# Two queues and two due times in a decoder layer: gate loads through POOL, pooled loads in ACT's order, two late channels

## The chip, the core and the metric

The kernel runs on one core of a Trainium2 chip. The core has a matrix engine (TensorE, PE), VectorE (DVE), ScalarE (ACT), GpSimd (POOL) and SyncE (SP), and 16 DMA engines that move data between its memories and HBM. Each engine takes its instructions in a fixed order; SP, ACT and POOL also issue DMAs, each from its own queue, in that order. The metric is the device time of one execution in microseconds, the median of several runs.

## The reference

One decoder layer over 1024 tokens with 2048 channels, in float32. One projection makes queries, keys, values, two gate channels sets and the pooled branch; two token mixers work on it; each branch is gated by a SiLU; an output projection and a gated embedding follow, and a layer norm.

```python
h = jnp.einsum('bsd,dc->bsc', x, w_in) + b_in
q, k, v, g_attn, u_pool, g_pool = jnp.split(h, SPLIT_POINTS, axis=-1)
a = banded_sink_attention(q, k, v, sinks, bias_hqk, valid) * jax.nn.silu(g_attn)
b = multiscale_pool(u_pool, w_pool, pool_scale) * jax.nn.silu(g_pool)
mix = jnp.einsum('bsc,cd->bsd', jnp.concatenate([a, b], axis=-1), w_out)
ple = jax.nn.sigmoid(jnp.einsum('bsd,de->bse', x, w_gate_ple)) * jnp.einsum('bsp,pd->bsd', p_i, w_ple)
return layer_norm(DEEPNORM_ALPHA * x + mix + ple, ln_gain, ln_bias)
```

`multiscale_pool` has four groups g of 256 channels with trailing windows of 2, 4, 8 and 16 tokens: window mean less the token itself, then a 256x256 map per group (w_pool) and a scale per channel.

## The kernel before, in words

**Products.** A float32 matrix product is made from high and low parts: each operand is cast to fp32r (`wh`, ACT, L222) and the rest is taken by a subtraction (`wl`, DVE, L122), and three matmuls stand for one (high by high L179, low by high L180, high by low L181). Activations are split in the same way into sets of operands b11, b21, t1, t2, t3, b22, t4 (`split_unit`, L242 to L250). The seven operands are those of a scheme with seven block products instead of eight. Each job makes two blocks of 128 output channels in such seven products; one product is 12 matmuls of 128x512. Where two jobs form a pair, their products alternate (14 products). Banks `qa` and `qb` of the accumulators are emptied by a copy on ACT (L346) or an addition on DVE (L348, shown as L122).

**Order.** After each product `tick` counts one up. `after(n, f)` calls f at the n-th product from now; `later(n, f)` does the same and also holds f's instructions behind the newest of PE, ACT and DVE. A scheduler then fixes the order of each engine's queue from the order of the code and its own costs. So a due time in products is a place in five queues.

**The stages around the change.** The second half of the projection's jobs comes last in its stage: gates and pooled channels (gp0, u0 in a pair; then gp3, u3, gp2, u2, u1, gp1), eight jobs of the embedding's gate (wgate), and the attention's gates ga0, ga1 and the pair ga2, ga3. When such a job ends (`finished`), POOL issues an accumulating load that adds the first half's sum (`part<-h`, or `part<-g` for wgate; L359), and `wait` products later `done` runs for each of its two channels:
- `gate_attn`: a Silu on ACT (L597), four products with `s<-pre` (loads of the attention's result) on DVE, and a store into `cc` on POOL's queue (`aside`, L141).
- `gate_pool`: a Silu (L604) and a store into `sgp` on SP's queue.
- `pool_u`: the window sums (ACT, DVE), and for the second channel of a group the loads of w_pool and of the gates `s<-sgp` (by `fetch` on SP's queue, L136), and `mix` with its matmuls (`sc`), the product with the gates (L653) and four stores into `cc` on POOL's queue.

The output projection reads `cc`: its pooled half (`cc4` to `cc7`, eight loads of 512 KB, `two<-cc`, L267) is loaded by `set_from`, whose steps then make the seven operands; this runs during ga1 and the pair ga2, ga3. The attention's half comes later in the same way. Waits of a DMA on a buffer or on a semaphore lane hold all that stands behind it in its issuer's queue.

Of the kernel before, what the change touches and what calls it, by code (L numbers as in the profile page):

```python
# [32 lines left out]
T = 512  # L33
# [21 lines left out]
class Job:  # L55


    def __init__(self, w, b0, b1, half, first, done, tokens=2 * T, plain=False, ahead=None):
        self.ahead, self.filled, self.mean, self.wait = ahead, False, False, 4
        self.w, self.b, self.half, self.first, self.done = w, (b0, b1), half, first, done  # L60
        self.tokens, self.plain = tokens, plain


class Layer:
# [74 lines left out]
    def aside(self, out, src):  # L139

        self.nc.gpsimd.dma_start(out=out, in_=src)  # L141

    def fetch(self, src, extra=False):
        s = self.extra() if extra else self.slot()
        return self.load(s[:, : src.shape[-1]], src)
# [109 lines left out]
    def set_from(self, get, F, keep=None, first=None, by=None):  # L255
# [4 lines left out]
        def fetch(u, part=None):  # L260
            h, k = int(u[2]) - 1, 2 * (int(u[1]) - 1)
            if not part:
                r[u] = [self.two() for _ in range(2)]
            for i, t in enumerate(r[u]):
                src = get(h, k + i)
                if part is None:
                    (by or (nc.sync if first else nc.scalar)).dma_start(out=t, in_=src)  # L267
                elif i == 0 and part < 2:
                    self.load(t[:, part], src[:, part])
                elif i == 1 and part == 2:  # L270
                    self.load(t, src)
# [13 lines left out]
        def begin():  # L285
# [4 lines left out]
            for i, u in enumerate(("b11", "b21", "b12", "b22")):  # L290
                self.later(1 + 2 * i, lambda u=u: fetch(u))
# [62 lines left out]
    def finished(self, job, i, t):  # L354
# [7 lines left out]
        self.later(job.wait, lambda: job.done(job.b[i], t))  # L362
# [245 lines left out]
    def pool_u(self, j, c):  # L608
# [24 lines left out]
        if j % 2:  # L633
# [4 lines left out]
            self.after(6 + late, lambda: self.got.update({("sg", g): [[self.fetch(self.sgp[2 * g + e][:, h * T : h * T + T]) for e in range(2)] for h in range(2)]}))  # L638
# [201 lines left out]
    def run(self):  # L840
# [63 lines left out]
        for j in s3:  # L904
            j.wait = 3 if j in s3[-2:] else 4
            j.ahead = self.embed_ahead if j.w is wgate else (lambda b: self.gate_ahead(b - GA0)) if j.b[0] < U0 and j.wait == 4 else None
        mixed = [(wout, *p) for p in pairs(0, 8)]
# [116 lines left out]
        pooled, *make_pooled = self.set_from(lambda h, k: self.cc[4 + k][:, :, h * T : h * T + T], T, by=nc.sync)  # L1024
        for i in range(n3):
# [7 lines left out]
            if i == n3 - 2:  # L1033
# [8 lines left out]
                for n, step in enumerate(make_pooled):  # L1042
                    self.after(10 + 3 * n, step)
# [187 lines left out]
```

## Time and profile before

| | |
|---|---|
| median of 3 runs | 1488.71 us (1487.96 to 1489.05) |
| the profiled execution | 1488.72 us |
| its span, first to last instruction | 1486.9 us |
| PE busy | 1447.6 us, 97% of the span |
| DVE, ACT, POOL busy | 1118.7 (75%), 779.5 (52%), 278.1 us (19%) |
| mean granted TensorE clock | 0.992 of full speed |

Busy time is what an engine worked; it says nothing on what it waited for. A busy PE is one whose matmuls follow each other. A row with "[2.21 <-ACT part L346]" tells that the engine stood idle for 2.21 us before it and that this ACT instruction ended the wait. L numbers are lines of the kernel before.

### The profile page before, as it was taken

The numbers are of one execution on the slowest core, as the hardware profiler recorded it, in microseconds if no ns is written. First come the engines' busy times: TensorE is split into PE (matmuls) and PEld (weight loads), VectorE is DVE, ScalarE is ACT, GpSimd is POOL, SyncE is SP. The second block draws the span as 40 slices with busy tenths as digits, with TensorE's granted clock in tenths as the row PEclk, the third lists the DMA queues.
The fourth block names the chain that finished last, engine by engine and source line by source line (L and its number), as shares of the span: only waits on it lengthen the run. The fifth ranks groups of instructions, "written<-read, shape, count | busy, mean of one in ns | idle before, by whom it ended". The sixth has DMA issues, their size and how long they took to land. (4 is left out here: it accounts for less than half of the span.)

```text
span 1486.9 us, 20458 instructions
## 1 busy us (share of the span) xinstructions
PE 1447.6 (97%) x6972; PEld 1223.5 (82%) x6972; DVE 1118.7 (75%) x2019; ACT 779.5 (52%) x1548; POOL 278.1 (19%) x388
## 2 busy tenths in 40 slices
PE   8999999999999999999999999999999999999996
PEld 6788888888887888888887778888877788899986
DVE  7788578888797878888667956565669666987786
ACT  5454666655666555666534443333256333554485
POOL 0000123332332333231111110000011111111231
PEclk9999999999999999999999999999999999999998
DMA  7563875445545455457856676666696768585464
GB/s 264 198 226 94 254 207 183 149 158 179 174 170 178 163 183 186 175 190 250 200 139 201 156 233 182 180 178 184 183 294 174 190 175 235 136 256 121 151 233 163
DMA packets 101913, 280.38 MB, mean 189 GB/s; under 512 B 11504, under 2 KB 17008, under 8 KB 101808
## 3 DMA queue, kind: packets, MB, share of 16 engines
q1 hardware_dynamic: 79024, 204.87, 40.3%
q0 software_dynamic: 19456, 66.86, 19.4%
q10 hardware_dynamic: 3328, 7.34, 1.5%
q8 instruction: 55, 0.90, 0.2%
q14 instruction: 50, 0.41, 0.1%
HBM read 193.04 MB, written 85.98 MB: 188 GB/s over the span
## 5 line engine op out<-in xcount | busy, mean ns | idle before, releaser
L222 ACT CAST wh<-raw 128x512 fp32r<-128x512 f32 x428 | 264.2, 619 | 448.6 <-PE qa L180 143.6
L122 DVE TENSOR_TENSOR wl<-raw,wh 128x512 fp32r<-128x512 f32 x428 | 299.5, 704 | 132.3 <-ACT wh L222 127.6
L346 ACT COPY part<-qa 128x512 f32<-128x512 f32 (+1 forms) x180 | 103.7, 576 | 56.5 <-PE qa L181 52.1
L551 POOL TENSOR_SCALAR_AFFINE_SELECT s<-s 128x512 fp32r<-128x512 f32 x128 | 100.6, 797 | 141.0 <-ACT s L544 98.3
L122 DVE TENSOR_TENSOR part<-part,qb 128x512 f32<-128x512 f32 (+1 forms) x120 | 80.9, 674 | 49.7 <-PE qb L181 47.0
L179 PE MATMUL qa<-b11h,wh 128*128 128x512 f32 (+2 forms) x292 | 111.2, 381 | 2.0 <-ACT b11h L248 1.5
L180 PE MATMUL qa<-b11l,wh 128*128 128x512 f32 (+2 forms) x292 | 110.2, 377 | 0.2 <-DVE b11l L122 0.2
L181 PE MATMUL qa<-b11h,wl 128*128 128x512 f32 (+2 forms) x292 | 109.8, 376 | 0.0
L179 PE MATMUL qb<-b21h,wh 128*128 128x512 f32 (+2 forms) x292 | 109.6, 375 | 0.0
L181 PE MATMUL qb<-b21h,wl 128*128 128x512 f32 (+2 forms) x292 | 109.2, 374 | 0.0
L180 PE MATMUL qb<-b21l,wh 128*128 128x512 f32 (+2 forms) x292 | 109.1, 374 | 0.0
L181 PE MATMUL qa<-t2h,wl 128*128 128x512 f32 (+1 forms) x260 | 100.0, 386 | 7.6 <-DVE wl L122 7.6
L179 PE MATMUL qa<-t2h,wh 128*128 128x512 f32 (+1 forms) x260 | 100.7, 388 | 5.3 <-ACT part L346 2.7
L179 PE MATMUL qb<-t1h,wh 128*128 128x512 f32 (+1 forms) x260 | 101.6, 391 | 3.5 <-DVE part L122 1.9
L181 PE MATMUL qb<-t1h,wl 128*128 128x512 f32 (+1 forms) x260 | 100.4, 386 | 1.5 <-DVE wl L122 1.5
L179 PE MATMUL qa<-t4h,wh 128*128 128x512 f32 (+1 forms) x260 | 100.3, 386 | 0.3 <-DVE part L122 0.3
L179 PE MATMUL qa<-t3h,wh 128*128 128x512 f32 (+1 forms) x260 | 100.5, 387 | 0.0
L180 PE MATMUL qb<-t1l,wh 128*128 128x512 f32 (+1 forms) x260 | 100.4, 386 | 0.0
L179 PE MATMUL qb<-b22h,wh 128*128 128x512 f32 (+1 forms) x260 | 100.3, 386 | 0.0
L180 PE MATMUL qb<-b22l,wh 128*128 128x512 f32 (+1 forms) x260 | 99.7, 384 | 0.0
L180 PE MATMUL qa<-t3l,wh 128*128 128x512 f32 (+1 forms) x260 | 99.7, 384 | 0.0
L181 PE MATMUL qb<-b22h,wl 128*128 128x512 f32 (+1 forms) x260 | 99.7, 383 | 0.0
(287 smaller groups left out, 3553.9 us busy)
## 6 DMA issues: line engine op xcount, KB each, us to landing
raw<-in_win SPq DMA_DIRECT2D x65, 512.0 KB, 4.0
h<-part SPq DMA_DIRECT2D x34, 512.0 KB, 2.9
part<-h POOLq DMA_DIRECT2D x34, 512.0 KB, 6.2
cw<-in_wout SPq DMA_DIRECT2D x64, 256.0 KB, 2.9
raw<-in_wgate SPq DMA_DIRECT2D x32, 512.0 KB, 4.4
raw<-wc SPq DMA_DIRECT2D x32, 512.0 KB, 4.1
s<-in_x SPq DMA_DIRECT2D x44, 256.0 KB, 5.7
wc<-cw SPq DMA_DIRECT2D x32, 256.0 KB, 2.3
```

What stands on the lines that cost most here:

```text
L122: return (eng or self.nc.vector).tensor_tensor(out=out, in0=a, in1=b, op=op)
L179: mm(ps, wh, xh, start=start, stop=False, skip_group_check=True)
L180: mm(ps, wh, xl, start=False, stop=False, skip_group_check=True)
L181: return mm(ps, wl, xh, start=False, stop=stop, skip_group_check=True)
L222: self.unit_latest = [nc.scalar.copy(out=hi, in_=src).ins, L.lo(lo, src, hi).ins]
L346: self.mark("ACT", self.nc.scalar.copy(out=dst, in_=ps))
L551: nc.gpsimd.affine_select(out=o4, in_=a4, pattern=[[0, 4], [sign, P]], compare_op=ALU.is_ge, fill=0.0, base=0 if side else -1, channel_mul ...
```

## The change

Four edits. The four gate loads `s<-sgp` of the group with g = 1 are issued from POOL's queue instead of SP's. The eight pooled loads are issued from ACT's queue instead of SP's, and their four steps, two loads each, become due at the 4th, 7th, 10th and 13th product from the start of ga1 instead of the 1st, 3rd, 5th and 7th. The steps that make operands of them become due one product later. And of the jobs of u2 and u3 the second channel is done two products later than the first (`apart`).

```diff
--- before.py
+++ after.py
@@ -56,7 +56,7 @@
 
 
     def __init__(self, w, b0, b1, half, first, done, tokens=2 * T, plain=False, ahead=None):
-        self.ahead, self.filled, self.mean, self.wait = ahead, False, False, 4
+        self.ahead, self.filled, self.mean, self.wait, self.apart = ahead, False, False, 4, 0
         self.w, self.b, self.half, self.first, self.done = w, (b0, b1), half, first, done
         self.tokens, self.plain = tokens, plain
 
@@ -139,10 +139,11 @@
     def aside(self, out, src):
 
         self.nc.gpsimd.dma_start(out=out, in_=src)
-
-    def fetch(self, src, extra=False):
+        return out
+
+    def fetch(self, src, extra=False, by=None):
         s = self.extra() if extra else self.slot()
-        return self.load(s[:, : src.shape[-1]], src)
+        return (by or self.load)(s[:, : src.shape[-1]], src)
 
     def split(self, src, extra=False):
         n = src.shape[-1]
@@ -252,7 +253,7 @@
     def two(self):
         return self.tile(self.twos, [P, 2, self.F], "two")
 
-    def set_from(self, get, F, keep=None, first=None, by=None):
+    def set_from(self, get, F, keep=None, first=None, at=(1, 2)):
 
         nc = self.nc
         r = {}
@@ -264,7 +265,7 @@
             for i, t in enumerate(r[u]):
                 src = get(h, k + i)
                 if part is None:
-                    (by or (nc.sync if first else nc.scalar)).dma_start(out=t, in_=src)
+                    (nc.sync if first else nc.scalar).dma_start(out=t, in_=src)
                 elif i == 0 and part < 2:
                     self.load(t[:, part], src[:, part])
                 elif i == 1 and part == 2:
@@ -288,7 +289,7 @@
                 first(fetch)
                 return
             for i, u in enumerate(("b11", "b21", "b12", "b22")):
-                self.later(1 + 2 * i, lambda u=u: fetch(u))
+                self.later(at[0] + at[1] * i, lambda u=u: fetch(u))
 
         def s0():
             if first:
@@ -359,7 +360,7 @@
         self.nc.gpsimd.dma_start(out=t, in_=job.first(job.b[i]), accum_op=ALU.add)
         if job.ahead:
             job.ahead(job.b[i])
-        self.later(job.wait, lambda: job.done(job.b[i], t))
+        self.later(job.wait + job.apart * i, lambda: job.done(job.b[i], t))
 
     def run_group(self, g, steps=(), then=None):
 
@@ -635,7 +636,8 @@
             self.after(4, lambda: self.got.update({("wp", g): self.fetch(self.wpool[g // 2][:, f])}))
             self.later(8, lambda: self.got.update({("wp", g): self.split(self.got["wp", g])}))
             late = 3 if g == 1 else 0
-            self.after(6 + late, lambda: self.got.update({("sg", g): [[self.fetch(self.sgp[2 * g + e][:, h * T : h * T + T]) for e in range(2)] for h in range(2)]}))
+            self.after(6 + late, lambda: self.got.update({("sg", g): [[self.fetch(self.sgp[2 * g + e][:, h * T : h * T + T], by=self.aside if g == 1 else None)
+                                                                     for e in range(2)] for h in range(2)]}))
             self.later(10 + late // 2, lambda: self.mix(g))
 
     def mix(self, g):
@@ -904,6 +906,8 @@
         for j in s3:
             j.wait = 3 if j in s3[-2:] else 4
             j.ahead = self.embed_ahead if j.w is wgate else (lambda b: self.gate_ahead(b - GA0)) if j.b[0] < U0 and j.wait == 4 else None
+        for j in s3:
+            j.apart = 2 if j.b[0] in (U0 + 4, U0 + 6) and j.w is win else 0
         mixed = [(wout, *p) for p in pairs(0, 8)]
         centred = [(self.wc, *p) for p in pairs(4, 6) + pairs(0, 2)]
         s4 = jobs(mixed, 1, lambda w: kept_part(self.r), lambda w: lambda b, c: self.co_done(b, c))
@@ -1021,7 +1025,7 @@
         g += n2
 
 
-        pooled, *make_pooled = self.set_from(lambda h, k: self.cc[4 + k][:, :, h * T : h * T + T], T, by=nc.sync)
+        pooled, *make_pooled = self.set_from(lambda h, k: self.cc[4 + k][:, :, h * T : h * T + T], T, at=(4, 3))
         for i in range(n3):
             if i == 1:
                 over.close()
@@ -1040,7 +1044,7 @@
                 self.twos = self.work_pool("twos1", 8, work)
                 pooled()
                 for n, step in enumerate(make_pooled):
-                    self.after(10 + 3 * n, step)
+                    self.after(11 + 3 * n, step)
                 for n, b in enumerate(b for j in s3[-2:] for b in j.b):
                     self.after(14 + 2 * n, lambda b=b: self.gate_ahead(b - GA0))
             self.run_group(g + i, () if i else steps)
```

Lines below the edits move by one to four numbers in the new file (L222 becomes L223, L267 L268, L597 L598).

The order of instructions moves in these places. First POOL's queue where the u1 and gp1 jobs' mixer (g = 1, `cc5`) meets the first wgate job; `cc6` are the stores of the mixer before it. Before:

```order
L141 DMA cc6_226<-s_1679_8408 128x512
L359 DMA part_1723_8603<-g_37_130 128x1024
L359 DMA part_1724_8604<-g_38_131 128x1024
L141 DMA cc5_225<-s_1746_8713 128x512
L141 DMA cc5_225<-s_1747_8715 128x512
L141 DMA cc5_225<-s_1748_8717 128x512
L141 DMA cc5_225<-s_1749_8719 128x512
```

and after:

```order
L141 DMA cc6_226<-s_1706_8497 128x512
L141 DMA s_1746_8713<-sgp_71_164 128x512
L141 DMA s_1747_8715<-sgp_72_165 128x512
L141 DMA s_1748_8717<-sgp_71_164 128x512
L141 DMA s_1749_8719<-sgp_72_165 128x512
L360 DMA part_1719_8567<-g_37_130 128x1024
L360 DMA part_1720_8568<-g_38_131 128x1024
L141 DMA cc5_225<-s_1746_8713 128x512
L141 DMA cc5_225<-s_1747_8715 128x512
```

The four loads that stood in SP's queue now stand ahead of the accumulating loads part<-g and the mixer's stores.

Second, the queues at the start of ga1. Before, SP issued the pooled loads, with `s<-pre` (the gates' loads of ga1) between them:

```order
L136 DMA raw_2051_10429<-in_wout 128x1024
L267 DMA two_2038_10358<-cc4_224 128x2x512
L267 DMA two_2039_10359<-cc5_225 128x2x512
L267 DMA two_2046_10407<-cc6_226 128x2x512
L267 DMA two_2047_10408<-cc7_227 128x2x512
L267 DMA two_2054_10448<-cc4_224 128x2x512
L267 DMA two_2055_10449<-cc5_225 128x2x512
L136 DMA s_2060_10487<-pre_63_156 128x512
L136 DMA s_2061_10489<-pre_63_156 128x512
L136 DMA s_2062_10492<-pre_64_157 128x512
L136 DMA s_2063_10494<-pre_64_157 128x512
L267 DMA two_2064_10496<-cc6_226 128x2x512
```

Now SP goes from raw<-in_wout to s<-pre at once, and the loads stand in ACT's queue. These are the rows of ACT from the second Silu of ga1's gates to the last two pooled loads; the first six stand ahead of them:

```order
L598 ACTIVATE part_2034_10339<-part_2034_10339,cst_75 128x1024
L223 CAST wh_2079_10572<-raw_1984_10035 128x512
L249 CAST b11h_2082_10590<-two_2048_10423 128x1024
L249 CAST b11h_2082_10590<-two_2049_10424 128x1024
L223 CAST wh_2084_10596<-raw_2017_10224 128x512
L347 COPY part_2063_10493<-qb_2086_10600 128x512
L223 CAST wh_2087_10614<-raw_2013_10202 128x512
L249 CAST b21h_2094_10653<-two_2060_10488 128x1024
L249 CAST b21h_2094_10653<-two_2061_10489 128x1024
L347 COPY part_2065_10495<-qb_2089_10618 128x512
L268 DMA two_2090_10632<-cc6_226 128x2x512
L268 DMA two_2091_10633<-cc7_227 128x2x512
```

The loads of b22 (`cc6`, `cc7`) are behind the copy into part_2065, the buffer that a store of a gate empties.

Third, DVE where the first pair of the output projection comes to its fifth product, with `part_2126<-part_2126,qb_2142` the step that empties the bank of the third product, and the gates of ga3 beside it (`part<-s,part`; part_2068, 2069 before, part_2064, 2065 after). Before:

```order
L122 TENSOR_TENSOR raw_2110_10732<-raw_2109_10730,raw_2110_10732 128x512
L122 TENSOR_TENSOR part_2126_10824<-part_2126_10824,qb_2142_10902 128x512
L122 TENSOR_TENSOR part_2068_10502<-s_2114_10753,part_2068_10502 128x512
L122 TENSOR_TENSOR part_2068_10502<-s_2115_10755,part_2068_10502 128x512
L122 TENSOR_TENSOR part_2069_10503<-s_2122_10801,part_2069_10503 128x512
L122 TENSOR_TENSOR part_2069_10503<-s_2123_10803,part_2069_10503 128x512
L122 TENSOR_TENSOR raw_2109_10730<-s1_2139_10893,raw_2109_10730 128x512
L122 TENSOR_TENSOR wl_2141_10899<-s1_2139_10893,wh_2140_10898 128x512
```

and after:

```order
L122 TENSOR_TENSOR s1_2139_10893<-raw_2108_10724 128x512
L122 TENSOR_TENSOR part_2064_10494<-s_2114_10753,part_2064_10494 128x512
L122 TENSOR_TENSOR part_2064_10494<-s_2115_10755,part_2064_10494 128x512
L122 TENSOR_TENSOR part_2065_10495<-s_2122_10801,part_2065_10495 128x512
L122 TENSOR_TENSOR part_2065_10495<-s_2123_10803,part_2065_10495 128x512
L122 TENSOR_TENSOR raw_2108_10724<-raw_2107_10722,raw_2108_10724 128x512
L122 TENSOR_TENSOR wl_2141_10899<-s1_2139_10893,wh_2140_10898 128x512
L122 TENSOR_TENSOR raw_2107_10722<-s1_2139_10893,raw_2107_10722 128x512
L122 TENSOR_TENSOR part_2126_10824<-part_2126_10824,qb_2142_10902 128x512
L122 TENSOR_TENSOR raw_2107_10722<-raw_2107_10722 128x512
```

The four gate products of ga3 and two steps of the weights (wl_2141 and the raw step behind it) stood behind part_2126 and now stand ahead of it.

## Rows read from the trace of the kernel before

**Rows 1.** The page: its first line, the engines in part 1 (busy us, share of the span, instructions), and one line of part 6 (DMA issues: KB each, median us to landing).

```profile
span 1486.9 us, 20458 instructions
...
PE 1447.6 (97%) x6972; PEld 1223.5 (82%) x6972; DVE 1118.7 (75%) x2019; ACT 779.5 (52%) x1548; POOL 278.1 (19%) x388
...
part<-h POOLq DMA_DIRECT2D x34, 512.0 KB, 6.2
```

**Rows 2.** The view of windows, core 0: us, then busy us (and instructions) of PE, PE's weight loads, DVE, ACT and POOL, then the granted TensorE clock, the DMA engines' share and GB/s.

```profile
760.00:832.00 72.00, 69.76 (x304) 56.10 (x303) 58.24 (x93) 33.17 (x59) 9.82 (x19) 1.00 0.61 161
...
872.00:900.00 28.00, 25.79 (x113) 20.88 (x112) 15.85 (x25) 10.55 (x17) 2.54 (x4) 1.00 0.63 195
900.00:1092.00 192.00, 192.00 (x840) 157.54 (x839) 113.26 (x176) 68.59 (x110) 14.69 (x18) 1.00 0.67 187
...
1112.00:1116.00 4.00, 4.00 (x12) 3.17 (x11) 4.00 (x5) 0.45 (x1) 0.00 (x0) 0.58 1.05 411
```

**Rows 3.** The view of waits, engine PE, between 760 and 1160 us: what waited for what, us in total, times, longest us.

```profile
PE qa L181 <- DVE wl L122: 4.3, 3, 3.4
PE qa L179 <- ACT wh L222: 2.5, 2, 1.5
PE qa L179 <- ACT part L346: 2.2, 1, 2.2
```

**Rows 4.** The timeline of PE around 881 us: start us, us, engine, line, operation, tiles (out<-in), shapes, count, [idle before <- what ended it].

```profile
878.78 0.39 PE L181 MATMUL qb<-b21h,wl 128*128 128x512 f32 x1
881.38 0.50 PE L179 MATMUL qa<-t2h,wh 128*128 128x512 f32 x1 [2.21 <-ACT part L346]
```

**Rows 5.** The chain of waits between 860 and 890 us: start us, us, what.

```profile
870.69 8.95 DMA cc<-s
```

**Rows 6.** The chain of waits between 1090 and 1120 us, in the same columns.

```profile
1094.40 10.19 DMA part<-h
...
1109.80 0.68 DVE wl L122
```

**Rows 7.** The timeline of PE at the fifth and sixth product of the first pair of the output projection.

```profile
1148.81 0.47 PE L179 MATMUL qb<-t1h,wh 128*128 128x512 f32 x1 [1.11 <-DVE part L122]
...
1154.71 0.50 PE L181 MATMUL qa<-t2h,wl 128*128 128x512 f32 x1 [0.42 <-DVE wl L122]
```

**Rows 8.** The timeline of PE behind the wait of 1107.

```profile
1106.74 0.39 PE L180 MATMUL qa<-t2l,wh 128*128 128x512 f32 x1
...
1111.47 0.39 PE L180 MATMUL qb<-t1l,wh 128*128 128x512 f32 x1
1111.70 0.40 PE L181 MATMUL qb<-t1h,wl 128*128 128x512 f32 x1
1111.94 0.59 PE L179 MATMUL qb<-t1h,wh 128*128 128x512 f32 x1
...
1115.58 0.39 PE L179 MATMUL qa<-t2h,wh 128*128 128x512 f32 x1
```

**Rows 9.** The timeline of SP's queue between 859 and 873 us (xN: issues taken together; us: from the first one's start to the last one's end).

```profile
865.15 2.48 SPq L136 DMA_DIRECT2D s<-sgp  x4
867.68 0.42 SPq L136 DMA_DIRECT2D s<-in_p  x1
```

**Rows 10.** The view of DMAs between 855 and 885 us: GB/s in 40 equal slices of the window, and issues with KB each and median us to landing.

```profile
GB/s 52 265 350 309 109 191 415 355 415 426 432 421 77 33 19 298 128 317 265 137 74 158 178 257 240 254 251 240 240 249 333 418 412 402 423 402 396 199 117 295
...
cc<-s POOLq DMA_DIRECT2D x5, 256.0 KB, 8.0
...
s<-sgp SPq DMA_DIRECT2D x4, 256.0 KB, 3.4
```

**Rows 11.** The timeline of POOL at the stores of the second gate pair.

```profile
1143.87 0.56 POOL L141 DMA_DIRECT2D cc<-part  x1 [4.77 <-DVE part L122]
1145.12 0.56 POOL L141 DMA_DIRECT2D cc<-part  x1 [0.69 <-issue]
```

**Rows 12.** The timeline of POOL between the s<-sgp loads and the mixer's first store.

```profile
867.05 0.90 POOL L359 DMA_DIRECT2D part<-g  x1 [11.29 <-DVE part L122]
869.48 0.88 POOL L359 DMA_DIRECT2D part<-g  x1 [1.53 <-ACT part L346]
```

**Rows 13.** The timeline of SP's queue between 1083 and 1110 us.

```profile
1083.81 8.12 SPq L267 DMA_DIRECT2D two<-cc  x6
...
1095.38 6.04 SPq L267 DMA_DIRECT2D two<-cc  x2
```

**Rows 14.** The timeline of ACT where the attention's half of cc is loaded from ACT's queue (ACTq).

```profile
1255.35 1.39 ACTq L267 DMA_DIRECT2D two<-cc  x1
```

**Rows 15.** The timeline of ACT at the second gate pair.

```profile
1148.08 0.58 ACT L346 COPY part<-qa 128x512 f32<-128x512 f32 x1 [3.81 <-DVE raw L122]
1148.56 2.19 ACT L597 ACTIVATE part<-part,cst 128x1024 f32<-128x1024 f32 x2
```

**Rows 16.** The timeline of DVE at the second gate pair.

```profile
1140.83 1.22 DVE L122 TENSOR_TENSOR b22l<-two,b22h 128x1024 fp32r<-128x1024 f32 x1
1141.96 2.49 DVE L122 TENSOR_TENSOR part<-s,part 128x512 f32<-128x512 f32 x4
...
1147.99 0.68 DVE L122 TENSOR_TENSOR part<-part,qb 128x512 f32<-128x512 f32 x1
```

**Rows 17.** The view of DMAs between 1080 and 1120 us.

```profile
cc<-part POOLq DMA_DIRECT2D x4, 512.0 KB, 6.9
```

## Prediction

> **What bounds the kernel now.** I read the page first. TensorE (PE) is busy 97% of a span of 1486.9 us [rows 1], so a change that adds and removes no work can only act on PE's waits. The windows then show where these lie: PE runs 192 us between 900 and 1092 without a gap, and loses time before and after it [rows 2]. The view of waits names them: three kinds make 9.0 us between 760 and 1160 us [rows 3]; with a smaller one at 1148.81 and a stretch at half clock, what the change can reach is some 12 to 15 us, 1% of the time.
>
> Three places matter. At 881.38 PE waits 2.21 us for a copy on ACT [rows 4]. The chain of waits leads back to one DMA, the store cc<-s of a pooling mixer, issued on POOL at 870.69 and landed 8.95 us later [rows 5]; its buffer is then rewritten by a cast on ACT, behind which stand a weight cast and the copy that PE needs. At 1107 PE waits 3.4 us for a weight's low part from VectorE (DVE); the chain there is an accumulating load part<-h of 10.19 us, then a Silu on ACT, four gate products on DVE, and the low part at 1109.80 [rows 6]. From 1148.81 on there are smaller waits [rows 7].
>
> **The price of the 1107 stall** is more than its wait. From the matmul at 1106.74 to that at 1115.58 there are 14 steps; at the steady 0.23 us (1111.47 to 1111.70, 0.227 before rounding) they would take 3.18 us, and they took 8.84: 5.66 us are lost. Of these 1.6 are the clock: nine steps from 1111.94 to 1115.58 took 3.64 instead of 2.04 [rows 8], and between 1112 and 1116 the granted clock was 0.58, most of the stretch at the level of 1.2 GHz [rows 2]. The wait of 2.21 us at 881 cost no clock: 872 to 900 shows 1.00.
>
> **Edit 1, gates through POOL.** Now SP issues four s<-sgp from 865.15 on, the first when its store has landed, and behind them the loads of p and x, from 867.68 [rows 9]. These then share the DMA engines with the stores that PE waits for: in this stretch cc<-s took 8.0 us by the median [rows 10]. With the four loads in POOL's queue, p and the first two x loads (768 KB) can go some 5 us sooner, right behind the sgp stores. The price is on POOL: behind the four loads stand two part<-g and then the cc<-s stores. A DMA costs POOL 0.56 us by itself and 1.25 from start to start with waits (1143.87 to 1145.12) [rows 11], so the four hold POOL for 2.2 to 5.0 us from 865.15 on, and part<-g, now at 867.05 and 869.48 [rows 12], follows. The first cc<-s store goes at 870.69 to 872.6. It lands at 876.0 at the earliest (872.6 and the 3.4 us of a s<-sgp load [rows 10]) and at 880.6 at the latest (872.6 and 8.0). I take 878.2, nearer to the measured 879.64: the backlog ahead is smaller by 768 KB, some 1.9 us at the 415 GB/s and more that the busy slices reach [rows 10]. PE resumed 1.74 us after the landing (881.38 less 879.64) and had been free since 879.17 (878.78 and 0.39 [rows 4]); at 878.2 a wait of 0.8 is left. Gain 1.4 us; bounds: a gain of 2.2 and a loss of 0.9.
>
> What the SP rows show is a queue that stands still: nothing leaves it until the first of the four loads may go at 865.15. The Trainium skill (DMA: Bandwidth & Descriptors, Issuing engines are not separate DMA queues) says that DMAs of all issuers run on the same 16 engines, so that another issuer saves issue time only. By that alone edit 1 would bring 0 and the sum below would stand 1.4 us later; the trace does not speak against the rule, but here the order in time changes with the issuer.
>
> The same store's 8.95 us can be set against that page's fit for a DMA issued on POOL (Anatomy of one DMA), 2.0 us and the bytes at 436 GB/s: an estimate of 2.6 us for 256 KB. By it the wait would be gone and the sum 0.8 us lower; the trace disagrees, as this store stands in a backlog.
>
> **Edit 3, the second channel later.** In the new order the window sums of the second channel keep their places on DVE and ACT; only the mixers' matmuls and weight splits come some ten matmuls later. So PE's losses between 760 and 832 (72.00 less 69.76, 2.24 us [rows 2]) stay: they end with DVE and with ACT behind DVE [rows 3]. Ten matmuls at 0.227 us delay the mixers' stores by 2.3 us, and those that wait for them are the next slots, not PE. I take 0; bounds: all 2.24 gained, or 1 us lost by the slots.
>
> **Edit 2, the pooled loads.** Eight loads of 512 KB leave SP, where six hold it for 8.12 us from 1083.81 and two for 6.04 from 1095.38, with the gates' s<-pre between and behind [rows 13]. On ACT one costs up to 1.39 us of its queue [rows 14], in all at most 11 us, spread over nine products of 2.7 us (12 steps of 0.227). The s<-pre of the first gate pair go 8 us sooner. The part<-h of 1094.40 meets two pooled loads at a time instead of a row of them, and lands in 6.2 us (the page's median [rows 1]) to 10.19 [rows 6], by 1100.6 to 1104.6. Then a Silu (1.1 us each, 2.19 for two [rows 15]), two products at 0.6, and the low part at 1104 to 1107 instead of 1109.80, where PE needs it at 1106.97. I take no wait and no half clock: 5.66 us gained here. If the load lands as late as now, a wait of up to 1.7 is left.
>
> Those 5.66 us are then largely given back. The fifth product of the next pair (qb<-t1h, at 1148.81 now [rows 7]) waits for DVE's part_2126, which empties the bank it writes. Before, that step stands ahead of the last four gate products; now it stands behind them and three more. In the new order 52 DVE instructions go from the first low part to it, 18 of 1024 columns (1.13 us a step, 1140.83 to 1141.96) and 34 of 512 (0.6, a quarter of the four that take 2.49) [rows 16]: 40.7 us. From 1105.5 that is 1146.2, and 1 us more for the last two pooled loads, which ACT issues behind a copy that waits for a store: 1147.2. A second chain lies beside it: the second pair of gates waits for a Silu, this for a copy, the copy for the landing of the first pair's store. The first pair's gates, behind 35 of the 52 (17 wide), end near 1137.9; the store goes 0.7 us later and the copy 4.2 after that (1143.87 to 1148.08 [rows 11, 15]); copy and two Silu take 2.7 (1148.08 to 1150.75), two gates and three steps 3.0. That is 1148.5, and PE starts 0.8 later (1147.99 to 1148.81): 1149.3.
>
> PE is there at 1147.7 (1148.81 less its wait of 1.11 [rows 7]) less 5.66, 1142.0. So a stall of some 7 us takes the place of that of 1107; three matmuls of the sixth product fill 0.7 of it. Against before: the fifth product starts 0.5 later, 0.7 of work is done ahead, and the losses that follow now go (1148.81 to 1154.71, 5.90 us for 16 steps of 0.227, so 2.3), since casts and products have had time. Half clock behind the new stall: 0 as after 881, 1.6 as after 1107, or twice that; I take 1.6, the nearer row. Sum of edit 2: 0.5 - 0.7 - 2.3 + 1.6 = -0.9 us. Bounds: with DVE's sum alone from 1104 (1144.7, PE at 1145.5) -4.7; with a store of 8 us and the longer half clock +4.6.
>
> **Sum.** -1.4 + 0 - 0.9 = -2.3 us. The profiled execution took 1488.72 us (its span and 1.8 around it) and the median of before is 1488.71, so the forecast is 1486.4. What a measurement of this kernel can tell from no change is 0.2%, 3.0 us: faster is below 1485.7, slower above 1491.7.
>
> **Rivals.** (A) DVE's own sum decides, not the store: the Silu are in time and the fifth product starts near 1145.5. For it: DVE has work for nearly the whole time here, and everything ahead of part_2126 comes earlier. Against: ACT's copy came 3.81 us late at 1148.08 [rows 15]; the view puts that down to a DVE step that ended just then, but the buffer that the copy fills is the one which the store of 1143.87 empties. Edit 2 is then -4.7 and edit 1 -1.4 to -2.2: 1481.8 to 1482.6. (B) Slower: the store cc<-part lands as late as its kin in the busy stretch, 6.9 us by the median [rows 17], or 8, instead of 4.1. The fifth product starts 2.8 to 3.9 later and the half clock lasts longer: edit 2 comes to +3.5 to +4.6, and edit 1 brings nothing or loses 0.9: 1492 to 1494. It decides from a landing after 6.5 us on. Against: 1136 and later is a calmer stretch for DMAs. (C) POOL's queue takes edit 1 back: the four loads wait for the sgp stores, cc<-s goes 2 us later and lands where it did: 1487.8. (D) Edit 3 does not do nothing, as the orders say, but frees PE's waits of 760 to 832: 2 us more, 1484.4.
>
> **Chances.** Forecast 0.50 (its own range 1484.5 to 1488.5), A 0.22, B 0.12, C 0.11, D 0.05. Of the forecast's half a quarter lies below 1485.7, with A and D: faster 0.40; C, the rest of the forecast and a little of B: same 0.46 or so; slower 0.14. The range that holds 8 in 10 is 1482.0 to 1491.0, with most of A inside and B outside.
>
> **What would show it.** Right: the wait at 1107 is under 0.5 us with the clock at 1.00 there; a wait of 5 to 7 us stands between 1140 and 1150 on DVE's part, with half clock after it; the wait at 881 is under 1.2; those between 760 and 832 are unchanged; L268 loads in ACT's queue take 0.5 to 1.4 us. Wrong: more than 1.7 us left at 1107, no long wait near 1145, or 2 us and more at 881 with cc<-s issued after 872.

## The result, and the profile after

The changed kernel takes 1495.87 us (median of 21 runs, 1490.21 to 1501.61) where the kernel before takes 1488.99 (21 runs on the same chip, 1487.45 to 1493.06): a ratio of 1.0040, 95% interval 1.0030 to 1.0049. It is slower by 0.4%, some 6 us. The profiled execution took 1493.30 us. Lines above the edits are one to two higher than before: L180 to L182 are the matmuls, L223 the casts of weights, L347 the copies, L598 the Silu of the attention's gates.

The page's first lines, and from its part 6 the accumulating loads (KB each, median us to landing), which stand against [rows 1]:

```profile
span 1491.5 us, 20466 instructions
...
PE 1450.2 (97%) x6972; PEld 1225.2 (82%) x6972; DVE 1118.7 (75%) x2019; ACT 779.7 (52%) x1548; POOL 280.6 (19%) x392
...
part<-h POOLq DMA_DIRECT2D x34, 512.0 KB, 6.9
```

The span is 4.6 us longer. PE's busy time grows by 2.6 us with as many matmuls, so some of them ran at a lower clock. The windows, with the columns of [rows 2], show where:

```profile
760.00:832.00 72.00, 69.78 (x304) 56.26 (x303) 59.01 (x94) 33.32 (x60) 9.73 (x18) 1.00 0.57 146
...
872.00:900.00 28.00, 24.96 (x102) 19.95 (x101) 13.81 (x23) 9.91 (x15) 2.40 (x4) 0.94 0.57 164
...
1112.00:1116.00 4.00, 4.00 (x19) 3.32 (x18) 4.00 (x6) 3.12 (x5) 0.00 (x0) 1.00 0.84 311
...
1136.00:1160.00 24.00, 17.07 (x61) 13.05 (x60) 20.07 (x30) 10.69 (x15) 3.29 (x6) 0.79 0.58 170
```

Between 1112 and 1116 the clock is now full and 19 matmuls run where 12 did. The loss has moved to two other places: 872 to 900, at a granted clock of 0.94, and 1136 to 1160, at 0.79. The waits of PE between 760 and 1160 us, against [rows 3]:

```profile
PE qa L180 <- ACT wh L223: 8.5, 3, 5.2
PE qa L180 <- ACT part L347: 3.0, 1, 3.0
PE qa L182 <- DVE wl L122: 1.0, 2, 0.5
PE qa L180 <- DVE part L122: 0.3, 1, 0.3
```

The wait on wl is down from 3.4 us to 0.5; the wait on ACT's copy, at 881, is up from 2.2 to 3.0; and one of 5.2 on a weight cast is new.

**The place at 881.** The chain of waits (start us, us, what) between 855 and 890, against [rows 5]:

```profile
859.55 7.14 DMA sgp<-part
...
870.61 9.42 DMA cc<-s
...
881.77 0.50 PE qa L180
```

POOL, against [rows 12]:

```profile
864.77 0.54 POOL L141 DMA_DIRECT2D s<-sgp  x1 [6.07 <-PE qb L182]
867.42 1.71 POOL L141 DMA_DIRECT2D s<-sgp  x3 [2.10 <-DMA s<-in_p]
869.20 1.82 POOL L360 DMA_DIRECT2D part<-g  x2
870.61 0.99 POOL L141 DMA_DIRECT2D cc<-s  x1
```

The four loads hold POOL from 864.77 to 869.13, and the store cc<-s goes at 870.61, 0.1 us from where it went before. It still lands at 880.03, a little later than before.

**The place at 1150.** The same view of the chain between 1125 and 1160:

```profile
1132.76 8.26 DMA part<-h
1141.02 5.29 DMA cc<-part
...
1149.28 1.28 DVE part L122 x2
1150.57 0.60 DVE raw L122
...
1152.46 0.63 ACT wh L223
...
1153.13 0.79 PE qa L180
```

DVE, ACT and PE there, against [rows 16], [rows 15] and [rows 7]:

```profile
1139.12 1.29 DVE L122 TENSOR_TENSOR part<-s,part 128x512 f32<-128x512 f32 x2
...
1148.07 2.50 DVE L122 TENSOR_TENSOR part<-s,part 128x512 f32<-128x512 f32 x4 [0.18 <-ACT part L598]
...
1152.29 0.68 DVE L122 TENSOR_TENSOR part<-part,qb 128x512 f32<-128x512 f32 x1
```

```profile
1146.41 0.59 ACT L347 COPY part<-qa 128x512 f32<-128x512 f32 x1 [2.53 <-DMA cc<-part]
1146.89 2.19 ACT L598 ACTIVATE part<-part,cst 128x1024 f32<-128x1024 f32 x2
1148.98 0.60 ACT L223 CAST wh<-s 128x512 fp32r<-128x512 f32 x1
1149.49 0.62 ACT L223 CAST wh<-raw 128x512 fp32r<-128x512 f32 x1
```

```profile
1150.16 0.79 PE L180 MATMUL qa<-t2h,wh 128*128 128x512 f32 x1 [5.18 <-ACT wh L223]
...
1153.13 0.79 PE L180 MATMUL qa<-t2h,wh 128*128 128x512 f32 x1 [1.76 <-ACT wh L223]
1153.72 0.63 PE L180 MATMUL qb<-t1h,wh 128*128 128x512 f32 x1
```

The first two gates (1139.12) end at 1140.4, and their store goes at 1141.02; that a part<-h landed at that moment, which the chain names, is chance, since the program lets the store wait for the gates. The store must land (1146.31) before ACT may copy into its buffer. Behind the copy stand two Silu, and behind these two things. On ACT it is the weight casts of 1148.98 and 1149.49, of which the second ends PE's wait of 5.18 us. On DVE it is the last four gate products (1148.07), and only behind them the steps of the weight, with the cast of 1152.46 that ends the wait of 1.76 us, and part_2126 (1152.29). Both waits are those of matmuls of the sixth product (qa<-t2h), three of which stand ahead of the fifth in PE's order. part_2126 ends at 1152.97 and ended neither wait; the fifth product (qb<-t1h) starts at 1153.72.

**The sum in the trace.** PE comes to the place of 1107 2.1 us later than before (1109.74 less its loss of 0.70, against 1110.54 less 3.57). There 5.66 less 0.70, 5.0 us, are won. At the fifth product 5.34 and 2.16 stand against 1.27, 1.15 and 0.59, and twelve steps at 0.43 instead of 0.23 add 2.4 to 2.5: 7.0 us lost. 2.1 - 5.0 + 7.0 = 4.1 of the span's 4.6.

### The profile page after: what moved, and what is told of

It reads as the page before. It is cut to its first block, busy times and chain, and to the rows that moved or that the text cites. A ratio compares the mean times of both kernels' runs of the same rounds, so it can differ in the third digit from the quotient of the medians.

```text
span 1491.5 us, 20466 instructions
## 1 busy us (share of the span) xinstructions
PE 1450.2 (97%) x6972; PEld 1225.2 (82%) x6972; DVE 1118.7 (75%) x2019; ACT 779.7 (52%) x1548; POOL 280.6 (19%) x392
## 5 line engine op out<-in xcount | busy, mean ns | idle before, releaser
L223 ACT CAST wh<-raw 128x512 fp32r<-128x512 f32 x428 | 264.3, 619 | 450.4 <-PE qa L181 143.3
L347 ACT COPY part<-qa 128x512 f32<-128x512 f32 (+1 forms) x180 | 103.7, 576 | 59.8 <-PE qa L182 54.0
L180 PE MATMUL qa<-t2h,wh 128*128 128x512 f32 (+1 forms) x260 | 102.6, 395 | 12.3 <-ACT wh L223 8.7
L180 PE MATMUL qa<-b11h,wh 128*128 128x512 f32 (+2 forms) x292 | 111.1, 381 | 2.1 <-ACT b11h L249 1.6
L182 PE MATMUL qa<-b11h,wl 128*128 128x512 f32 (+2 forms) x292 | 109.9, 377 | 0.0
L180 PE MATMUL qb<-b21h,wh 128*128 128x512 f32 (+2 forms) x292 | 109.2, 374 | 0.0
L182 PE MATMUL qb<-b21h,wl 128*128 128x512 f32 (+2 forms) x292 | 108.6, 372 | 0.0
L182 PE MATMUL qa<-t2h,wl 128*128 128x512 f32 (+1 forms) x260 | 101.5, 391 | 4.3 <-DVE wl L122 4.3
L180 PE MATMUL qb<-t1h,wh 128*128 128x512 f32 (+1 forms) x260 | 101.7, 391 | 1.7 <-DVE part L122 0.8
L182 PE MATMUL qb<-t1h,wl 128*128 128x512 f32 (+1 forms) x260 | 100.7, 387 | 1.5 <-DVE wl L122 1.5
L181 PE MATMUL qa<-t2l,wh 128*128 128x512 f32 (+1 forms) x260 | 101.0, 389 | 0.0
L180 PE MATMUL qa<-t4h,wh 128*128 128x512 f32 (+1 forms) x260 | 100.4, 386 | 0.3 <-DVE part L122 0.3
L180 PE MATMUL qa<-t3h,wh 128*128 128x512 f32 (+1 forms) x260 | 100.5, 387 | 0.0
L180 PE MATMUL qb<-b22h,wh 128*128 128x512 f32 (+1 forms) x260 | 100.3, 386 | 0.0
L182 PE MATMUL qa<-t4h,wl 128*128 128x512 f32 (+1 forms) x260 | 99.7, 383 | 0.0
```

The costliest lines, as they stand in the source:

```text
L180: mm(ps, wh, xh, start=start, stop=False, skip_group_check=True)
L181: mm(ps, wh, xl, start=False, stop=False, skip_group_check=True)
L182: return mm(ps, wl, xh, start=False, stop=stop, skip_group_check=True)
L223: self.unit_latest = [nc.scalar.copy(out=hi, in_=src).ins, L.lo(lo, src, hi).ins]
L347: self.mark("ACT", self.nc.scalar.copy(out=dst, in_=ps))
```

## The experiments

Losses in this section are the time from one matmul to the next, less the 0.227 us of a steady step; "h" says that the windows 864 to 896, 1096 to 1128 or 1136 to 1168 show a granted clock under 1.00 (0.84 to 0.95). Ratios are to the kernel before, measured beside it on the same chip, with the 95% interval. The third column has the losses between 864 and 890.

| run | ratio | near 881 | at 1107 | at the fifth product |
|---|---|---|---|---|
| before | 1 | 2.38 | 3.57 h | 1.27, 1.15, 0.59 |
| the change | 1.0040 (1.0030 to 1.0049) | 3.21 h | 0.70 | 5.34, 2.16 h |
| e1_gates_pool | 0.9975 (0.9961 to 0.9989) | none | 3.74 h | 1.27, 1.16, 0.59 |
| e2_pooled_act | 1.0042 (1.0027 to 1.0058) | 2.29 h | 2.30, 0.86 h | 5.24, 2.16 h |
| e3_apart | 1.0000 (0.9984 to 1.0015) | 2.55 h * | 2.67 | 1.27, 1.15, 0.59 |
| e23_no_edit1 | 1.0025 (1.0010 to 1.0040) | 2.71 | none | 5.59, 2.16 h |
| e12 | 1.0010 (0.9996 to 1.0024) | none | 2.00, 0.86 h | 5.25, 2.21 h |
| e13 | 1.0015 (1.0002 to 1.0027) | 5.05 h | 0.61, 3.06 h | 1.27, 0.95 |
| after_gates_late | 0.9995 (0.9981 to 1.0009) | 3.74 h | none | 3.90 h |
| e12_gates_late | 0.9973 (0.9959 to 0.9987) | none | 2.42, 0.86 h | 3.45 h |
| after_turn | 0.9993 (0.9979 to 1.0008) | 0.91 * | 0.80 | 6.10, 2.16 h |
| after_turn_gates_late | 0.9972 (0.9955 to 0.9988) | 0.61 * | none | 3.98 h |
| before_turn | 0.9969 (0.9953 to 0.9986) | none | 3.63 h | 1.27, 1.15, 0.59 |
| e12_steps_10 | 0.9995 (0.9983 to 1.0006) | none | 2.80 h | 4.14, 0.79 h |

"None" is no loss over 0.5 us. A star marks another wait than that of 881: it lies at 870 to 873, where a matmul of the mixer (`sc`) waits for a product with the gates on DVE.

### Each edit alone, and the change without one of them

**e1_gates_pool**, edit 1 alone:

```diff
-[self.fetch(self.sgp[...]) for e in range(2)]
+[self.fetch(self.sgp[...], by=self.aside if g == 1 else None) for e in range(2)]
```

> Edit 1 alone. Own places (each edit's loss sits where it acts): the first cc<-s store lands at 880 or later, PE's wait at 881 stays 2.2 to 3.2 us, the stall of 3.4 us at 1107 and the wait of 1.1 at 1149 stay as before; time +0.5 to +3 us. Together only (the loss needs edit 3, which lets PE arrive 0.8 us earlier): the wait at 881 is 2.2 us or less without half clock, time within 0.5 us of before.

Measured 1486.50 us, 3.9 under the kernel before beside it; neither expectation held. The wait at 881 is gone, but not because the store got faster. In this stretch (855 to 885, view of DMAs) cc<-s takes longer than the 8.0 us of [rows 10], and the first one, issued at 871.19, landed at 881.19:

```profile
cc<-s POOLq DMA_DIRECT2D x5, 256.0 KB, 9.3
```

ACT's cast of p, which waited for that landing before, starts without any wait:

```profile
873.69 0.62 ACT L670 CAST s<-s 128x512 fp32r<-128x512 f32 x1
```

So the cast writes another buffer. In before it gets, by the program, the buffer of s_1746, which the store empties; with edit 1 it gets another one of the 16 slots. The traces leave the numbers of the buffers out, so this is a reading of the program until the runs with a memset below test it: moving the four loads in the order had moved the turn in which the pool hands its buffers out.

**e2_pooled_act**, edit 2 alone:

```diff
-self.later(1 + 2 * i, lambda u=u: fetch(u))
+self.later(at[0] + at[1] * i, lambda u=u: fetch(u))
-pooled, *make_pooled = self.set_from(..., T, by=nc.sync)
+pooled, *make_pooled = self.set_from(..., T, at=(4, 3))
-    self.after(10 + 3 * n, step)
+    self.after(11 + 3 * n, step)
```

> Edit 2 alone. Own places: 1107 falls to under 1 us of loss, a new stall of 5 to 8 us at the fifth product of the output projection (about 1143 to 1151) with half clock behind it, time +1 to +4 us. Together only: the new stall is there but under 5 us, since nothing before it is late, time 0 to -2 us.

Measured 1496.65 us, 6.2 over before: the whole loss of the change by itself, and more than either expectation. The new stall is there in full, and that of 1107 is only half gone.

**e3_apart**, edit 3 alone:

```diff
-self.later(job.wait, lambda: job.done(job.b[i], t))
+self.later(job.wait + job.apart * i, lambda: job.done(job.b[i], t))
+for j in s3:
+    j.apart = 2 if j.b[0] in (U0 + 4, U0 + 6) and j.w is win else 0
```

> Edit 3 alone. Own places: the waits of 784, 819 and 829 stay within 0.3 us each, the wait at 881 stays 2.2, time within 0.7 us of before. Together only: the mixers that come later move POOL's stores, and the wait at 881 grows to 3 us with half clock, time +2 us or more.

Measured 1489.97 us, no difference; the waits between 760 and 832 are those of before. The expectation for 881 was missed: PE has no wait there. It stands earlier, at 872.94, for a product with the gates, which waits on DVE for a load:

```profile
872.13 0.75 DVE L653 SCALAR_TENSOR_TENSOR s<-sc,cst,s 128x512 f32<-128x512 f32 x1 [2.51 <-DMA s<-sgp]
```

The cast of p waits for cc<-s here as in before (3.34 us, to 878.12); PE comes too late to feel it.

**e23_no_edit1**, the change without edit 1 (the diffs of the two runs above):

> Edits 2 and 3 without edit 1. Own places: the wait at 881 is 2.2 us with a clock of 1.00 as before, the stall at the fifth product stays, time +1 to +4 us over before, 2 to 4 us under the changed kernel. Together only: time as the changed kernel or as before, not between.

Measured 1494.64 us, 4.2 over before, with the waits of the first expectation. Without edit 1 the change loses 0.25%, with it 0.40%. The two differ by less than their uncertainty (some 0.2%), but an edit that wins 0.25% alone wins nothing here. So the next two runs put edit 1 beside one other edit at a time.

**e12**, edits 1 and 2:

> Edits 1 and 2 without edit 3. Buffer theory (with edit 1 alone the cast in front of PE's copy at 881 gets a buffer that the mixers' matmuls free instead of the one that the store cc<-s empties, and edit 3 changes the turn of the buffers back): the wait at 881 is gone here as with edit 1 alone (under 0.3 us), the new stall of 5 to 8 us near 1148 stays; time 3 to 6 us under the changed kernel, +0 to +3 over before. Traffic theory (edit 1 gains because p and x loads leave earlier): the same wait of 2 to 3 us as in the changed kernel, time as the changed kernel.

**e13**, edits 1 and 3:

> Edits 1 and 3 without edit 2. Buffer theory: the cast waits for cc<-s again, landed at 880 or later, a wait of 2.2 to 3.2 us at 881, and the gain of edit 1 alone is lost: within 1.5 us of before. Traffic theory: the gain of edit 1 stays, 3 to 4 us under before.

Measured 1492.75 and 1493.82 us; e12 came out as the buffer theory expected. Against the same kernel without it, edit 1 gives -0.25% alone and -0.32% beside edit 2 (1.0010 against 1.0042), but +0.15% beside edit 3 and +0.15% beside both. Each of these differences is uncertain by some 0.2%, so the two gains are clear of it and the two losses are not; that edit 1 gains less beside edit 3 is. They fall by one rule: of the kernels with edit 1 and no memset, those without edit 3 have no wait of PE at 881, those with it lose 3.2 to 5.1 us. In e13, whose loss there (5.05 us) and time (2.4 us over before) are above what was expected, POOL and ACT show it:

```profile
870.37 0.95 POOL L141 DMA_DIRECT2D cc<-s  x1
```

```profile
881.63 0.62 ACT L670 CAST s<-s 128x512 fp32r<-128x512 f32 x1 [8.94 <-DMA cc<-s]
```

With edit 3 the slots are asked for in another order, and the cast has the buffer of s_1746 again. Edit 2 costs in all four places: +0.42, +0.35, +0.25 and +0.25%.

### DVE's order at the fifth product

**after_gates_late** and **e12_gates_late**: the change, and edits 1 and 2, with the gates of ga3 done six products after their job, not three:

```diff
-j.wait = 3 if j in s3[-2:] else 4
+j.wait = 6 if j in s3[-1:] else 3 if j in s3[-2:] else 4
```

> The changed kernel with the last job's gates (ga3) done 6 products after it instead of 3, nothing left out. Order theory (the new stall is DVE's: the step that empties the bank of the fifth product stands behind the last four gate products, which wait for two Silu and a store): that step now stands ahead of them, the stall near 1150 falls from 7.5 us to under 2.5, without half clock; time 5 to 9 us under the changed kernel, 0 to 3 under before. Rival, DVE's own load (the sum of its steps sets the end, whatever their order): a stall of 4 us or more stays, or comes back one product later; gain under 3 us.

> Edits 1 and 2 without edit 3, with ga3's gates after 6 products. If both theories hold, the waits at 881, 1107 and 1149 are all under 1.5 us: 8 to 12 us under before, 13 to 17 under the changed kernel. If only the order theory holds: 3 to 6 us more than that. If only the buffer theory holds: about as edits 1 and 2 alone.

Measured 1489.73 us for the first: 0.9995 instead of 1.0040. DVE, PE and ACT:

```profile
1148.47 0.68 DVE L122 TENSOR_TENSOR part<-part,qb 128x512 f32<-128x512 f32 x1
```

```profile
1149.30 0.77 PE L180 MATMUL qb<-t1h,wh 128*128 128x512 f32 x1 [3.74 <-DVE part L122]
```

```profile
1154.68 2.19 ACT L598 ACTIVATE part<-part,cst 128x1024 f32<-128x1024 f32 x2
```

part_2126 now stands ahead of the last four gate products and starts at 1148.47 instead of 1152.29; PE loses 3.90 us once instead of 5.34 and 2.16. The time is as the order theory expected; the stall is over its 2.5 us, with half clock behind it, and near the rival's 4. The second kernel, 1487.04 us, gains nearly as much (1.0010 to 0.9973); its waits of 2.3 us at 1107 and 3.3 at the fifth product and its 4.4 us under before miss what was expected if both theories hold. In the medians the late gates give back all that edit 2 costs. But the edit moves more than part_2126: on ACT the two Silu now stand behind the weight casts (1154.68, where they were at 1146.89), and in PE's order the fifth product stands ahead of the sixth. How much of the gain is DVE's order and how much ACT's these two runs can't tell; nor was the kernel before timed with the late gates, which may win there as well. What is left is a row of DVE steps without a gap from 1143.11 on, behind two gates whose Silu waited for a part<-h.

**e12_steps_10**: edits 1 and 2 with the steps due as in before, which also puts part_2126 ahead of the last four gates.

```diff
-self.after(11 + 3 * n, step)
+self.after(10 + 3 * n, step)
```

> Edits 1 and 2, but the steps that make operands stay due at the 10th product from the start of ga1 instead of the 11th. DVE's order at the second gate pair is then that of before: the step that empties the bank stands ahead of the last four gate products. Order theory: the fifth product's wait is as before, under 3 us with the small ones behind it, and no half clock; the time is 0.9955 to 0.9985 of before, near that with the gates late (0.9973). Rival (the loads' place in ACT's queue and the late store, not the order, make the new stall): a wait of 4 us or more stays and the time is that of edits 1 and 2, 0.9995 to 1.0020.

Measured 1489.99 us, 0.9995: the expectation of the order theory, under 3 us, was missed, and time and wait are at the edge of what the rival expected. Here the two Silu stay ahead of the weight casts on ACT (1147.78). The second wait of PE is down to 0.79, the first is 4.14. The chain and PE:

```profile
1133.06 9.08 DMA part<-h
...
1142.46 4.74 DMA cc<-part
```

```profile
1149.06 0.47 PE L180 MATMUL qb<-t1h,wh 128*128 128x512 f32 x1 [3.98 <-ACT part L598]
```

The view puts the wait down to a Silu; what PE needs is the bank, and part_2126 ends at 1148.9. The accumulating load sets the start of the first pair's second gates, and part_2126 is the seventh DVE step behind these two. So two things make the new stall: the place of the last four gates, with their Silu on ACT, and a DVE chain that hangs on part<-h and cannot follow PE when PE comes earlier.

### The turn of the buffers

**after_turn** and **before_turn**: the changed kernel and the kernel before with one instruction more. It takes a slot just ahead of the cast and writes 16 columns of it on POOL; every other instruction is that of the kernel it is added to. (The last two lines are there already; the first is cut short.)

```diff
+for _ in range(1 * h * k):
+    self.nc.gpsimd.memset(self.slot()[:, :16], 0.0)
 hi, lo = (...(F32R)[:, :T] for i in range(2))
 self.nc.scalar.copy(out=hi, in_=r_)
```

> The changed kernel with one memset of 128x16 on POOL more, into a slot that is taken just ahead of the cast of p near 881; no other instruction is added or moved. The memset takes the buffer that the store cc<-s of s_1746 reads, and the cast gets the next one. Theory (the turn of the buffers holds PE at 881, not the time at which the store lands): the wait of 3 us at 881 is gone although the store lands no earlier; with the half clock behind it that is 3 to 5 us, 1490.5 to 1492.5, 0.997 to 0.998 of the changed kernel. The new stall at the fifth product stays, 4 to 8 us. Rival (the stores' traffic holds PE there in any case): a wait of 2 us or more stays between 872 and 886 on another load, and the time stays within 0.1% of the changed kernel.

> The kernel before with the memset alone. If edit 1 won by the buffer alone, this wins as much: the wait of 2.2 us at 881 is gone, 0.9975 to 0.9990. The memset stands between the second and the third store of cc<-s on POOL and holds those behind it some 8 us, which the next loads into their buffers may show. If edit 1 won by the traffic, this brings nothing: 0.9995 to 1.0005.

Measured 1490.97 and 1486.01 us. POOL and ACT of after_turn:

```profile
873.21 0.92 POOL L141 DMA_DIRECT2D cc<-s  x1
...
882.80 0.11 POOL L671 MEMSET s<- 128x16 f32 x1 [7.87 <-DMA cc<-s]
```

```profile
875.58 0.62 ACT L673 CAST s<-s 128x512 fp32r<-128x512 f32 x1
```

Now the memset waits 7.87 us for the store's landing at 882.75, where PE does not need it, and the cast goes at 875.58. The two stores behind the memset wait with it (to 883.40), and no wait of PE comes of that. The store took 9.5 us, longer than the 8.95 of [rows 5], and PE no longer waits for it. The waits of PE between 860 and 1160 in after_turn, and in before_turn:

```profile
PE qa L180 <- ACT wh L223: 7.7, 2, 5.9
PE sc L180 <- DVE s L655: 0.7, 1, 0.7
PE qa L182 <- DVE wl L122: 0.6, 1, 0.6
```

```profile
PE qa L181 <- DVE wl L122: 3.9, 2, 3.5
PE qb L179 <- ACT part L346: 1.1, 1, 1.1
PE qa L179 <- ACT wh L222: 1.0, 1, 1.0
```

The wait for ACT's copy at 881 is in neither. One memset gives 0.9969 on the kernel before, as much as edit 1 (0.9975, the intervals overlap): the four loads' queue had no part in edit 1's gain that these runs can tell. Both medians gain more (3.9 and 4.9 us) than the 2.4 us that the trace of before loses at 881.

**after_turn_gates_late**: the changed kernel with both remedies.

> The changed kernel with the memset of the run before and with the gates of ga3 done six products after their job instead of three. If the two causes, the buffer at 881 and DVE's order at the fifth product, make up the loss, both are out: no wait over 1 us at 881, one of 3 to 4.5 at the fifth product, 1485.5 to 1488, ratio to before 0.9970 to 0.9985, as edits 1 and 2 with the gates late had (0.9973). If a third thing holds the changed kernel back (edit 3), 1489 or more.

Measured 1485.73 us, 0.9972 of before. Its waits of PE over the same stretch:

```profile
PE qb L180 <- DVE part L122: 4.1, 2, 3.8
PE sc L180 <- DVE s L655: 0.4, 1, 0.4
```

With both remedies nothing of the loss is left. Each remedy alone brings 0.45 to 0.47%, both 0.68% (uncertain by some 0.2% each), and the wait at 881 was there before the change too. With both out it beats the kernel before by as much as before_turn does; that one is the smallest edit of those that win.

## Why the prediction was wrong, point by point

**The forecast** was 1486.4 us, the range to 1491.0; the result, 1495.87, is outside. Two terms of the sum failed.

**Edit 1, forecast -1.4 us.** The step "I take 878.2" failed: the store landed at 880.03. It rested on a backlog smaller by 768 KB. POOL's issue time was sized rightly (4.4 us of 2.2 to 5.0, the store at 870.61), but p and x, sent ahead (from 859.97 on), now ran beside the sgp stores: the second of these took 7.14 us where it took 6.06 before, and landed at 866.69 where it landed at 866.31. The mixer's store then took 9.42 us instead of 8.95. The bytes were the same, in another order. Rival C had the outcome, a store that lands where it did, but not the way (the store went no later) and not the price: half clock followed the wait, and PE was 2.1 us late at 1107. In the runs with edit 1 the store took 8.3 to 11.2 us and landed at 879.5 to 882.8, no earlier than before by more than 0.2. On this the Trainium skill (DMA: Bandwidth & Descriptors, Issuing engines are not separate DMA queues), by which another issuer saves issue time only, was the better guide, and the runs agree with it.

Behind this lies what the prediction did not ask at all: why the cast waits for that store. It took the buffer as given, and it is the one thing that decides: -0.25% where the turn falls well, +0.15% (no loss beyond the uncertainty) where edit 3 turns it back. Alone the edit won 3.7 us (0.25% of 1489), more than the bound of 2.2.

**Edit 3, forecast 0.** Right in time: alone 1.0000, waits between 760 and 832 as before, rival D is out. In the trace it is luck in part: a new loss of 2.55 us at 872.94 stands where that of 881 was, and 1107 loses 2.67 without half clock where it lost 3.57 with it. And "the next slots, not PE" looked only at when slots come free and not at which slot comes next, and so missed that edits 1 and 3 aren't independent: a sum of single terms could not come out.

**Edit 2, forecast -0.9, bounds -4.7 to +4.6.** With what was measured, in before's time, the same sum reads 2.8 - 0.7 - 2.3 + 2.4 = +2.2 us (the trace's 7.0 less 5.0 above): the fifth product started 2.8 later and not 0.5, the half clock took 2.4 and not 1.6, and the other two terms held.

The first half came true: at 1107 the wait is 0.5 us and the clock 1.00. But the reason given, a part<-h that lands early, did not: it took 9.99 us there, inside the forecast's 6.2 to 10.19 but at its end. That the wait went all the same is luck. In before it was not the Silu that held the four gate products. DVE before:

```profile
1107.23 2.65 DVE L122 TENSOR_TENSOR part<-s,part 128x512 f32<-128x512 f32 x4 [3.48 <-DMA s<-pre]
```

They waited for their loads s<-pre, which stood behind the pooled loads in SP's queue and landed from 1107.14 on (this wait is not on the chain of [rows 6]). In the change these land by 1092.2, and each two products follow their Silu:

```profile
1104.66 1.29 DVE L122 TENSOR_TENSOR part<-s,part 128x512 f32<-128x512 f32 x2
1107.79 1.29 DVE L122 TENSOR_TENSOR part<-s,part 128x512 f32<-128x512 f32 x2 [1.84 <-ACT part L598]
```

The prediction saw that s<-pre would go 8 us sooner and gave it no part in the wait.

The second half had the right place and the right chain (the store, the copy, two Silu, the last four gates, half clock behind) and too small a size. The forecast put the fifth product at 1149.3 in before's time; it came at 1153.72, which is 1151.6 less the 2.1 us that PE was already late. Of the 2.3 us too many, 1.1 is the store (it landed 5.29 us after its issue, where the forecast let the copy go 4.2 after it), 0.4 the first gates, 0.2 DVE's steps and 0.6 the start of PE. Here the step "three matmuls of the sixth product fill 0.7 of it" failed: it took them for work that was free to run. Both of PE's waits, 5.18 and 1.76, are theirs, for weight casts on ACT. The wait of 5 to 7 us that was to stand on DVE's part stood on ACT's, and ended at 1150.16. Rival A is out, since the copy did wait for the store (2.53 us). Rival B named the side and the place; its condition, a store landing after 6.5 us or more, did not come true. It was several steps, each a little later. Alone, edit 2 lost 0.42%, 6.2 us, more than its bound.

**What is open.** The median of the change lies 6.9 us above that of before, the profiled execution's span only 4.6, and its 21 runs spread over 11 us where those of before spread over 6. What the longer executions lose, no trace here shows. The stall at 1107 goes fully with edits 2 and 3 together and only by half without edit 3 (2.00 to 2.80 and more). The traces show where: the second part<-h of ga1 took 12.3 to 13.1 us in the four runs with edit 2 and without edit 3, and 9.6 to 10.4 in the five with both. Why it takes longer is open. So is what the late gates would bring in the kernel before.

## What to carry to other kernels

Where an engine waits for a store only because a pool hands its buffer on, ask which buffer comes next before weighing the store: an edit that moves requests in the order can move the turn, so edits that look independent can add up wrongly, and one request of a few columns, written on an idle engine, tests it and may be the whole remedy. A step that empties an accumulator's bank, and a weight cast that PE needs next, belong ahead of steps that hang on a DMA; when PE is freed earlier at one place, compute when the slowest chain of the next place can follow, from the landing that starts it. Where several edits come together, time each alone and with each other before explaining their sum.

## What the runs showed of the hardware

A wait of PE of one length was followed by half clock in some runs and not in others: after losses of 2.29 us (e2, at 877.9) and 2.55 (e3, at 872.9) the granted clock fell, to 0.95 over the 32 us from 864 on, and after 2.38 (before, at 881.4) and 2.71 us (e23, at 882.1) it stayed at 1.00. A saving of a microsecond at such a place can therefore be worth some 1.6 more (an estimate, the price of the half clock at 1107 in before), or nothing.

The issue of a DMA of 512 KB from ACT's queue cost 0.53 us by the median here, and 0.75 at most, where the prediction had reckoned with up to 1.39 [rows 14]. In the view of line L268 in the change (duration ns min/median/max, first and last start):

```profile
L268 ACTq DMA_DIRECT2D two<-cc x8: 525/532/754, 1089.5 to 1114.3; - x8
```

A wait of such an issue comes on top: that of 1102.90 stood until an earlier two<-cc had landed at 1102.88, and the Silu behind it on ACT started at 1103.47, after 1.54 us idle.
